# Chaining the second MLP product in PSUM over two quarters, with its finish dealt out and its operand buffers shared

## The chip, the cores and the metric

The kernel runs on one core of a Trainium2 chip. The metric is the device time of one execution in microseconds (us), as the median of several runs.

## What is computed

The reference is one layer of a hybrid diffusion backbone over 2048 tokens of width 1024: token mixing (long convolutions, a state space model, pooling, attention), an output projection, and an MLP. The change concerns the MLP and what ends the layer:

```python
def sq_relu_mlp(h, w1, w2):
    return jnp.square(jax.nn.relu(h @ w1)) @ w2
...
    fl = sq_relu_mlp(modulate(rmsnorm(xl, lp["norm_pre_mlp"]), mod_l[3], mod_l[4]), lp["mlp_w1"], lp["mlp_w2"])
    xl = xl + mod_l[5] * rmsnorm(fl, lp["norm_post_mlp"])
```

Here `h` is 2048 x 1024, `w1` 1024 x 4096 and `w2` 4096 x 1024, all in float32.

## The kernel before

**Precision.** A float32 product is made of three matmuls. `split` (L663) rounds an operand to a high part on ScalarE (L666) and makes the low part by a subtraction on VectorE or GpSimd (L669). `mm3` (L672) issues high x high, high x low and low x high (L674, L675, L676).

**Seven products for eight.** Both MLP products are cut into 2 x 2 blocks and computed with seven block products and additional sums and differences (a Strassen-Winograd scheme). The differences of the weights are made on the chip while the product runs; for the second product the seven left operands are made by the first and kept in DRAM as `m_d`.

**The first product, `mlp_up`** (L1273), runs over two halves of the tokens and 16 chunks each. It holds its right operands as split tiles: `he` (needed early in a chunk, in the pool `hh` on the right side of SBUF) and `hb` (later). TensorE writes PSUM tiles named X, Y, Z; `total` (L1302 to L1304) adds a kept sum on VectorE and squares the positive part on ScalarE. The end of a chunk makes four sums on VectorE (L1361) and writes seven blocks to `m_d` (L1369).

**The output projection, `mix_out`** (L1143), runs before it, block by block of 128 tokens, and its last transposition `turn(7)` is followed by `mlp_up`.

**The second product, `mlp_down`** (L1390). For each half of the tokens and each of eight quarters q of the inner dimension (each 512 deep) it loads two 1 MB pieces of `w2` (`raw`, L1424), makes the differences t1 to t4 (`summed2`, L1493, on VectorE or GpSimd), and calls `product` seven times. `product` loads the left operand (`mr`, L1438), splits it (`ms`) and the weights (`w2s`), and runs 24 matmuls of 128x512: twelve (two token blocks, two 128-deep steps k, three of `mm3`) into each of two PSUM tiles `ps` of two banks. So a quarter has 7 x 24 = 168 matmuls, a half 8 x 168, the stage 2688. Every `ps` is brought out at once: copied by ScalarE in the first quarter (L1450), added to `acc` by VectorE in the others (L1452). Which engine makes which low part is written out in the calls (V is VectorE, G GpSimd).

**The finish.** In the last quarter of a half the seven sums are combined (L1463 to L1486, VectorE and GpSimd), and `finish` (L1404) is called on each y: squares and their sums on ScalarE (L1409), the root by a chain of small VectorE ops (`rsqrt`, L638 to L647), then per 128 tokens a load of x (L1415), the scaling on VectorE (L1416), the addition of x on GpSimd or VectorE (L1417), and the store (L1418).

**Order.** The program is written in the order of these calls; each engine takes its instructions in its own order, and a tile is free when its last reader is done. SP issues all loads and stores of this stage, in order. `psum` has four two-bank tiles in `mlp_down`, and six `ps` and two `pt` one-bank tiles in the stage before it, under separate pools, so the pools of the second product open when those of the first close.

Of the kernel before, what the change touches and what calls it, by code (L numbers as in the profile page):

```python
# [9 lines left out]
F32 = mybir.dt.float32  # L10
F32R = mybir.dt.float32r
# [1131 lines left out]
def mix_out(nc, tc, psum, PI, H, a, C, w, rows_d, cols_d, mT_d, x1_d, h2_d, t_d, raw):  # L1143
# [3 lines left out]
    with tc.tile_pool(name="mo", reuse_waits="tile", bufs=1, side="right") as P:  # L1147
        rows = load(nc, P, rows_d[:, 0], "rows0")
        cols = load(nc, P, cols_d, "colsl")
        def block(blk):  # L1150
            ts = slice(128 * blk, 128 * blk + 128)
            m = PI.tile([128, 8, 128], F32, name="m", bufs=2)
            nc.sync.dma_start(m, mT_d[:, :, ts])
            mh = PI.tile([128, 2, 8, 128], F32R, name="mh", bufs=2)
            split(nc, m, mh[:, 0], mh[:, 1], nc.scalar, V)
            x = P.tile([128, D], F32, name="xr", bufs=2)
            nc.sync.dma_start(x, a["x"][ts])
            ps = [psum.tile([128, 512], F32, tag="ps", name="ps") for _ in range(2)]
            for h in range(2):
                hs = slice(512 * h, 512 * h + 512)  # L1160
                for k in range(8):
                    mm3(nc, ps[h], mh[:, 0, k], mh[:, 1, k], wh[:, k, hs], wl[:, k, hs], k == 0, k == 7)
            rs = P.tile([128, 1], F32, name="ors", bufs=4)
            row_rstd(nc, P, ps, rs, "ro")
            y = P.tile([128, D], F32, name="x1", bufs=2)
            for h in range(2):
                hs = slice(512 * h, 512 * h + 512)
                V.scalar_tensor_tensor(y[:, hs], ps[h], rs, rows[:, hs], op0=ALU.mult, op1=ALU.mult)
            G.tensor_tensor(y, y, x, ALU.add)
            nc.sync.dma_start(x1_d[ts], y)  # L1170
            rs2 = P.tile([128, 1], F32, name="ors2", bufs=4)
            row_rstd(nc, P, [y[:, 0:512], y[:, 512:1024]], rs2, "ro")
            xn = P.tile([128, D], F32, name="xn", bufs=3)
            nc.scalar.activation(xn, y, AF.Copy, scale=rs2)
            return xn

        def turn(t, xs):
            for k in range(0, 8, 2):
                ps = psum.tile([128, 2, 256], F32, tag="pt", name="pt", bufs=2)
                for i in range(2):  # L1180
                    for j in range(2):
                        nc.tensor.transpose(ps[:, i, 128 * j:128 * j + 128], xs[j][:, 128 * (k + i):128 * (k + i) + 128], C["id"])
                for i in range(2):
                    h = P.tile([128, 256], F32, name="h2", bufs=3)
                    nc.scalar.activation(h, ps[:, i], AF.Identity, bias=cols[:, 0, k + i:k + i + 1], scale=cols[:, 1, k + i:k + i + 1])
                    nc.sync.dma_start(h2_d[:, k + i, 256 * t:256 * t + 256], h)

        xs, hb = {}, {}
        for blk in range(16):
            if blk == 12:  # L1190
                for t in raw:
                    nc.sync.dma_start(t[0], t[1])
            xs[blk] = block(blk)
            if blk % 2 == 0 and blk:
                turn(blk // 2 - 1, [xs[blk - 2 + i] for i in range(2)])
            if blk in (9, 10, 11, 12):
                mlp_first(nc, P, H, h2_d, t_d, blk - 9, hb)
# [510 lines left out]
```

## Time and profile before

| | us |
|---|---|
| median of 3 runs | 2978.19 (2974.49 to 2979.24) |
| the profiled execution, its time | 2975.95 |
| its span in the profile | 2974.2 |
| TensorE busy (PE) | 2719.0, 91% |
| VectorE busy (DVE) | 2165.1, 73% |
| GpSimd busy (POOL) | 1512.1, 51% |
| ScalarE busy (ACT) | 1392.7, 47% |
| mean granted clock of TensorE | 0.956 of full speed |

PE is TensorE's matmuls, PEld its weight loads, which overlap them; DVE is VectorE, ACT ScalarE, POOL GpSimd, SP the engine that issues transfers. Busy shares are averages over stages with different limits. The last stage, `mlp_down`, stretches from 2267 to 2974 us. A window row gives, for a stretch of the span, each engine's busy time and its instructions, the granted clock of TensorE (1.00 is 2.4 GHz, 0.50 is 1.2 GHz), the share in which the DMA engines were busy, and the rate. Some per cent of matmul records can be missing from a trace.

### The profile page before, as it was taken

The numbers are of one execution on the slowest core, as the hardware profiler recorded it, in microseconds if no ns is written. First come the engines' busy times: TensorE is split into PE (matmuls) and PEld (weight loads), VectorE is DVE, ScalarE is ACT, GpSimd is POOL, SyncE is SP. The second block draws the span as 40 slices with busy tenths as digits, with TensorE's granted clock in tenths as the row PEclk, the third lists the DMA queues.
The fourth block names the chain that finished last, engine by engine and source line by source line (L and its number), as shares of the span: only waits on it lengthen the run. The fifth ranks groups of instructions, "written<-read, shape, count | busy, mean of one in ns | idle before, by whom it ended". The sixth has DMA issues, their size and how long they took to land.

```text
span 2974.2 us, 38945 instructions
## 1 busy us (share of the span) xinstructions
PE 2719.0 (91%) x13228; PEld 2170.8 (73%) x13228; DVE 2165.1 (73%) x3946; ACT 1392.7 (47%) x2353; POOL 1512.1 (51%) x1334
## 2 busy tenths in 40 slices
PE   7979999978999889989998899999998999889993
PEld 3667778767775785878886677778886888668882
DVE  6867786379776887987677644464445789999997
ACT  5644223234864654647234545565555433353332
POOL 5856887366522622634114354444443555755555
PEclk9988999989999989989999999999999999989997
DMA  6454453253131411412565744464335444455432
GB/s 212 139 176 134 136 153 103 76 161 91 61 108 42 138 41 44 142 56 69 184 215 180 260 170 146 155 212 150 143 144 214 161 145 152 134 193 168 156 121 99
DMA packets 228486, 415.13 MB, mean 140 GB/s; under 512 B 35118, under 2 KB 97394, under 8 KB 226687
## 3 DMA queue, kind: packets, MB, share of 16 engines
q1 hardware_dynamic: 228287, 412.63, 42.7%
q8 instruction: 105, 1.72, 0.2%
q14 instruction: 94, 0.77, 0.1%
HBM read 277.90 MB, written 134.64 MB: 139 GB/s over the span
## 4 chain that ended last, share of the span: by engine, by line
PE 56%; DVE 13%; DMA 5%; issue 3%; ACT 3%; POOL 3%; SPq 0%; DVEq 0%; ACTq 0%; POOLq 0%
PE ps L675 8%; PE ps L676 8%; PE ps L674 8%; PE X L674 3%; PE X L675 3%; PE po L1003 3%; PE X L676 3%; PE pS L916 3%; PE pT L990 3%; PE ps L212 2%; PE Z L674 2%; PE Z L676 2%; PE Z L675 2%; DMA hl<-h_d 1%; DVE pt L669 1%
## 5 line engine op out<-in xcount | busy, mean ns | idle before, releaser
L675 PE MATMUL ps<-w2s,ms 128*128 128x512 f32 x896 | 353.4, 395 | 21.0 <-DVE w2s L669 20.2
L674 PE MATMUL ps<-w2s,ms 128*128 128x512 f32 x896 | 351.4, 395 | 18.0 <-DVE acc L1452 13.4
L676 PE MATMUL ps<-w2s,ms 128*128 128x512 f32 x896 | 351.5, 393 | 1.9 <-POOL ms L669 1.9
L666 ACT ACTIVATE ms<-mr 128x1024 fp32r<-128x1024 f32 x112 | 119.2, 1065 | 324.7 <-issue 146.9
L1452 DVE TENSOR_TENSOR acc<-ps,acc 128x1024 f32<-128x1024 f32 x196 | 234.3, 1214 | 33.4 <-PE ps L676 32.9
L669 POOL TENSOR_TENSOR ms<-mr,ms 128x1024 fp32r<-128x1024 f32 x64 | 162.3, 2536 | 150.7 <-ACT ms L666 150.6
L916 PE MATMUL pS<-KT,QT 128*128 128x512 f32 (+1 forms) x640 | 209.6, 420 | 17.1 <-DVE p L923 13.8
L923 DVE TENSOR_SCALAR_CACHE_REDUCE p<-pS 128x512 f32<-128x512 f32 (+1 forms) x320 | 198.0, 629 | 36.7 <-PE pS L916 34.0
L675 PEld LDWEIGHTS ps<-w2s,ms 128*128 128x128 f32 x896 | 170.7, 191 | 60.6 <-DVE w2s L669 23.0
L930 ACT ACTIVATE p<-p,mx 128x1024 f32<-128x1024 f32 (+1 forms) x192 | 177.4, 927 | 75.8 <-DVE mx L927 75.5
L674 PEld LDWEIGHTS ps<-w2s,ms 128*128 128x128 f32 x896 | 170.4, 190 | 56.4 <-issue 10.5
L669 POOL TENSOR_TENSOR w1s<-w1r,w1s 128x512 fp32r<-128x512 f32 x96 | 133.4, 1391 | 152.9 <-ACT w1s L666 151.3
L666 ACT ACTIVATE pt<-pT 128x512 fp32r<-128x512 f32 x256 | 146.3, 594 | 137.3 <-PE pT L990 119.6
L1003 PE MATMUL po<-pt,VV 128*128 128x256 f32 x1024 | 199.0, 309 | 11.7 <-DVE pt L669 7.0
L676 PEld LDWEIGHTS ps<-w2s,ms 128*128 128x128 f32 x896 | 170.6, 190 | 38.2 <-POOL ms L669 2.8
L990 PE MATMUL pT<-ident,p 128*128 128x128 f32 x1152 | 181.6, 279 | 9.9 <-DVE pt L669 4.6
L669 DVE TENSOR_TENSOR pt<-pT,pt 128x512 fp32r<-128x512 f32 x256 | 171.7, 683 | 18.1 <-ACT pt L666 16.4
L1003 PEld LDWEIGHTS po<-pt,VV 128*128 128x128 f32 x1024 | 154.1, 197 | 41.2 <-DVE pt L669 14.2
L669 DVE TENSOR_TENSOR w1s<-w1t,w1s 128x512 fp32r<-128x512 f32 x128 | 103.4, 810 | 110.0 <-ACT w1s L666 109.2
L990 PEld LDWEIGHTS pT<-ident,p 128*128 128x128 f32 x1152 | 138.6, 143 | 37.4 <-issue 18.0
L669 DVE TENSOR_TENSOR w2s<-w2t,w2s 128x1024 fp32r<-128x1024 f32 x64 | 135.5, 2117 | 25.8 <-ACT w2s L666 25.3
L1302 DVE TENSOR_TENSOR mu<-Z,pk 128x512 f32<-128x512 f32 x64 | 44.1, 690 | 146.1 <-ACT pk L1297 116.8
(484 smaller groups left out, 7767.8 us busy)
## 6 DMA issues: line engine op xcount, KB each, us to landing
mr<-m_d SPq DMA_DIRECT2D x112, 512.0 KB
w1r<-mlp_w SPq DMA_DIRECT2D x64, 512.0 KB
m_d<-mt SPq DMA_DIRECT2D x128, 256.0 KB
w2r<-mlp_w SPq DMA_DIRECT2D x32, 1024.0 KB
mw<-mod_w SPq DMA_DIRECT2D x96, 256.0 KB
m_d<-mu SPq DMA_DIRECT2D x96, 256.0 KB
kk<-k_d SPq DMA_DIRECT2D x128, 128.0 KB
hl<-h_d SPq DMA_DIRECT2D x48, 256.0 KB
```

The costliest lines, as they stand in the source:

```text
L212: nc.tensor.matmul(ps, lhsT=d1[0:64], rhs=zq[:, :, 16 * j:16 * j + 16].rearrange("p t c -> p c t"), start=True, stop=True)
L666: nc.scalar.activation(hi, src, AF.Copy)
L669: lo_eng.tensor_tensor(lo, src, hi.bitcast(F32), ALU.subtract)
L674: nc.tensor.matmul(out, lhsT=lh, rhs=rh, start=start, stop=False, skip_group_check=onto)
L675: nc.tensor.matmul(out, lhsT=lh, rhs=rl, start=False, stop=False, skip_group_check=onto)
L676: nc.tensor.matmul(out, lhsT=ll, rhs=rh, start=False, stop=stop, skip_group_check=onto)
L916: nc.tensor.matmul(s[:, :n], lhsT=QT[:, h, i], rhs=KT[j][:, :n], start=i == 0, stop=i == 1)
L923: V.tensor_scalar(p[:, c0:c0 + n], s[:, :n], 1.0, -3.0e38, op0=ALU.mult, op1=ALU.max, accum_out=mx[:, j:j + 1])
L930: nc.scalar.activation(p[:, :n], p[:, :n], AF.Exp, bias=mx[:, 5:6], accum_out=sm[:, j:j + 1])
L990: nc.tensor.transpose(tp[:, b, h], pr[h][c][:, 128 * i:128 * i + 128], C["id"])
L1003: nc.tensor.matmul(o, lhsT=VV[kb], rhs=pt[:, i, b], start=kb == 0 and i == 0, stop=kb == NB - 1 and i == 1)
L1452: V.tensor_tensor(acc[p][j], ps, acc[p][j], ALU.add)
```

## The change

`mlp_down` is written anew; the places around it change with its buffers.

- Two quarters are one pair. A product is four one-bank sums of 128x512, each chained in PSUM over both quarters of the pair (24 matmuls each where it stood at 12). Four banks are X and four are Z, all eight together; products 0, 5, 6, 3 go into X, products 1, 4, 2 into Z, and some continue a sum that is there (0, 5, 6, 3 and 4, 2 chain), so that several sums of the scheme come out of PSUM ready made. A sum is then copied by ScalarE (L1493, first pair) or added by VectorE (L1495), in pieces of 128x512.
- All low parts, all differences of weights (`minus`, L1435) and the whole finish of half 0 are on VectorE.
- The finish is a generator: `square_sum` (L1440, L1441), `root` (L1447, L1448) and `result` (L1463) per 128 tokens. Half 0's finish is handed out in half 1's first pair, three steps behind each product. Half 1's upper rows are finished between its last products, with the multiplications on GpSimd; its lower rows go block by block in the last product (`outer=True`, `after=end`).
- Operands of both products are `he` tiles from one pool of eight of [128, 2, 2, 512]; the left operands are loaded into `w1r` tiles on both sides of SBUF, the weights in 512 KB pieces.
- In `mix_out` the pool `mo` stays open, `turn(7)` is called in `mlp_up` behind the first two chunks' `begin` and `middle`, the first two `block`s of W1 are put into tiles of `mo`, and h is loaded in pairs.

The core of the diff:

```diff
-    with tc.tile_pool(name="mo", reuse_waits="tile", bufs=1, side="right") as P:
...
-        turn(7, [xs[14 + i] for i in range(2)])
-        return hb
+    return hb, lambda: turn(7, [xs[14 + i] for i in range(2)])
...
     for c in range(2):
         begin(c)
         middle(c)
+    left()
...
+    bank = lambda tag, b: psum.tile([128, 512], F32, tag=tag, name="acc" + tag, bufs=b)
+    pt = [psum.tile([128, 2, 256], F32, tag="pt", name="pt", bufs=2).rearrange("p a b -> p (a b)") for _ in range(2)]
+    ps = [psum.tile([128, 512], F32, tag="ps", name="ps") for _ in range(6)]
+    X, Z = pt + ps[0:2], ps[2:6]
 
-    def block(src, name, lo):
-        w = Q.tile([128, 2, 2, 512], F32R, name=name, bufs=3)
-        split(nc, src, w[:, 0], w[:, 1], A, lo)
+    def block(src):
+        w = H.tile([128, 2, 2, 512], F32R, name="he", bufs=8)
+        split(nc, src, w[:, 0], w[:, 1], A, V)
         return w
...
+    def m_block(half, p, q):
+        t = RW[loads[0] // 2 % 2].tile([128, 8, 128], F32, name="w1r", bufs=2).rearrange("p a b -> p (a b)").rearrange(
+            "p (k n) -> p k n", k=2)
+        loads[0] += 1
+        nc.sync.dma_start(t, m_d[half, p, :, 2 * q:2 * q + 2])
+        return t
...
+    def finish(half, t, acc, xs=(None,) * 4, eng=V):
+        ss = Q.tile([128, 2, 4], F32, name="mss", bufs=2)
+        for b in range(4):
+            for h in range(2):
+                square_sum(acc[t, h][b], ss[:, h, b:b + 1], h, eng)
+            yield
+        rs = root(ss, 4, "4")
+        for b in range(4):
+            result(1024 * half + 512 * t + 128 * b, [acc[t, h][b] for h in range(2)], rs[:, b:b + 1], xs[b])
+            yield
...
+            def product(p, w, dst, start, keys, outer=False, after=None):
+                ms = [None, None]
+                ws = [None, None]
+                steps = [(b, i) for b in range(4) for i in range(2)] if outer else [(b, i) for i in range(2) for b in range(4)]
+                for b, i in steps:
+                    if ms[i] is None:
+                        ms[i] = block(m_block(half, p, qs[i]))
+                        ws[i] = block(w[i])
+                    ts = slice(128 * b, 128 * b + 128)
+                    m, u = ms[i], ws[i]
+                    for k in range(2):
+                        mm3(nc, dst[b], m[:, 0, k, ts], m[:, 1, k, ts], u[:, 0, k], u[:, 1, k],
+                            start and i == 0 and k == 0, i == 1 and k == 1, not start)
+                    if i == 1:
+                        for key in keys:
+                            add(key, dst, b)
+                        if after:
+                            after(b)
+                for _ in range(3 if half == 1 and pair == 0 else 2):
+                    next(rest, None)
+
+            b11 = [w_block(q, 0, 0) for q in qs]
+            product(0, b11, X, True, [(0, 0)])
+            b21 = [w_block(q, 1, 0) for q in qs]
+            product(1, b21, Z, True, [(0, 0)])
...
+            product(5, t2, X, False, [(0, 1)])
+            product(4, t1, Z, True, [(1, 1)])
...
+                product(6, t3, X, False, [(1, 1)])
+                product(2, b22, Z, False, [(0, 1)])
+                product(3, t4, X, False, [(1, 0)])
+        if half == 0:
+            rest = both(finish(half, 0, acc), finish(half, 1, acc))
...
-    with pool("hh", side="right") as H, pool("w1r", side="right") as RW, pool("psC", bufs=6, space=PS) as psum:
+    with pool("w1r", side="right") as RW, pool("hh", side="right") as H, pool("psC", bufs=6, space=PS) as psum:
...
-    with pool("dr", side="right") as R, pool("md") as Q, pool("psD", bufs=4, space=PS) as psum:
-        mlp_down(nc, tc, psum, R, Q, a, rows_d, x1_d, m_d, a["out"])
...
+                with pool("md") as Q:
+                    mlp_down(nc, tc, psum, (RW, RQ), RQ, H, Q, a, rows_d, x1_d, m_d, a["out"])
```

TensorE's order where the first product ends and the second begins. Before, the last chunk's Z is done before the first `ps` (the operands of the second product are w2s and ms):

```order
L674 MATMUL Z<-hb,w1s 128x512
L675 MATMUL Z<-hb,w1s 128x512
L676 MATMUL Z<-hb,w1s 128x512
L674 MATMUL ps<-w2s,ms 128x512 x4
L675 MATMUL ps<-w2s,ms 128x512
L676 MATMUL ps<-w2s,ms 128x512
```

No matmul of the second product stands ahead of the first product's last. Now the new product's matmuls on `pt` and `ps`, with both operands in `he`, stand before the last chunk's X:

```order
L674 MATMUL pt<-he 128x512
L675 MATMUL pt<-he 128x512
L676 MATMUL pt<-he 128x512
L674 MATMUL ps<-he 128x512
L675 MATMUL ps<-he 128x512
L676 MATMUL ps<-he 128x512
L674 MATMUL X<-hb,w1s 128x512
L675 MATMUL X<-hb,w1s 128x512
L676 MATMUL X<-hb,w1s 128x512
```

Fifteen matmuls of the second product stand there, and further ones between the last X, X and Z of the first: 37 ahead of its last matmul.

VectorE's order where half 0 ends and half 1 begins. Before, in the last quarter of half 0, the combination and `finish` (L1476, L1481, L1410, L642) stand in one place with the accumulations:

```order
L669 TENSOR_TENSOR ms<-mr,ms 128x1024
L669 TENSOR_TENSOR w2s<-w2t,w2s 128x1024
L1452 TENSOR_TENSOR acc<-ps,acc 128x1024 x3
L1476 TENSOR_TENSOR y<-y,acc 128x2x512
L1481 TENSOR_TENSOR acc<-acc 128x1024
L1452 TENSOR_TENSOR acc<-ps,acc 128x1024
L1476 TENSOR_TENSOR y<-y,acc 128x2x512
L1410 TENSOR_SCALAR mss<-mss 128x2
L1481 TENSOR_TENSOR acc<-acc 128x1024
L1452 TENSOR_TENSOR acc<-ps,acc 128x1024
L642 TENSOR_SCALAR rmt<-mss 128x2
```

The splits of ms and w2s for the next products follow these rows. Now the multiplications of the finish (L1441) stand between additions and splits of half 1's first products:

```order
L669 TENSOR_TENSOR he<-w1r,he 128x1024
L1495 TENSOR_TENSOR acc<-ps,acc 128x512
L669 TENSOR_TENSOR he<-w2a,he 128x1024
L1495 TENSOR_TENSOR acc<-ps,acc 128x512
L1441 TENSOR_TENSOR acc<-acc,rows_21765 128x512
L1495 TENSOR_TENSOR acc<-ps,acc 128x512
L1441 TENSOR_TENSOR acc<-acc,rows_21765 128x512
L1495 TENSOR_TENSOR acc<-ps,acc 128x512
L1441 TENSOR_TENSOR acc<-acc,rows_21765 128x512
L669 TENSOR_TENSOR he<-w1r,he 128x1024
L669 TENSOR_TENSOR he<-w2a,he 128x1024
L1441 TENSOR_TENSOR acc<-acc,rows_21765 128x512 x4
```

The ops of the finish have moved from half 0's last quarter to half 1's first products, one to four at a time between the splits of `he`.

At the program's end VectorE now has the addition, the multiplication and the root chains of single blocks, two chains interleaved, and the fused multiply-adds (L1463) behind them:

```order
L1495 TENSOR_TENSOR acc<-ps,acc 128x512
L1441 TENSOR_TENSOR acc<-acc,rows_21765 128x512
L1448 TENSOR_SCALAR mv_26042<-mv_26042 128x1
L642 TENSOR_SCALAR rm1t<-mv_26007 128x1
L1441 TENSOR_TENSOR acc<-acc,rows_21765 128x512
L642 TENSOR_SCALAR rm1t<-mv_26042 128x1
L643 TENSOR_SCALAR mrs_26008<-rm1t 128x1
L643 TENSOR_SCALAR mrs_26043<-rm1t 128x1
```

The addition of the last of the four blocks is followed by two chains for two blocks; the other two blocks' chain and their L1463 come behind the first pair's.

## Rows read from the trace of the kernel before

**Rows 1.** The page's busy times of each engine over the whole span.

```profile
PE 2719.0 (91%) x13228; PEld 2170.8 (73%) x13228; DVE 2165.1 (73%) x3946; ACT 1392.7 (47%) x2353; POOL 1512.1 (51%) x1334
```

**Rows 2.** Windows: stretch, engines' busy time and instructions, clock, DMA share, GB/s.

```profile
2263.00:2304.00 41.00, 28.81 (x106) 21.69 (x105) 22.68 (x13) 22.18 (x24) 20.37 (x8) 0.83 0.64 236
2304.00:2560.00 256.00, 256.00 (x1132) 212.01 (x1131) 222.49 (x157) 100.20 (x100) 133.50 (x55) 1.00 0.48 155
2560.00:2680.00 120.00, 92.70 (x370) 73.32 (x369) 116.22 (x103) 52.01 (x61) 82.47 (x29) 0.87 0.47 167
...
2928.70:2974.20 45.50, 0.14 (x1) 0.00 (x0) 35.90 (x68) 7.20 (x14) 13.43 (x5) 0.54 0.44 162
```

**Rows 3.** Timeline of TensorE's last matmuls: start, duration, engine, line, tiles.

```profile
2925.73 0.39 PE L676 MATMUL ps<-w2s,ms 128*128 128x512 f32 x1
...
2928.45 0.39 PE L676 MATMUL ps<-w2s,ms 128*128 128x512 f32 x1
```

**Rows 4.** The page's costliest groups: busy, mean ns, idle before, releaser.

```profile
L675 PE MATMUL ps<-w2s,ms 128*128 128x512 f32 x896 | 353.4, 395 | 21.0 <-DVE w2s L669 20.2
...
L666 ACT ACTIVATE ms<-mr 128x1024 fp32r<-128x1024 f32 x112 | 119.2, 1065 | 324.7 <-issue 146.9
L1452 DVE TENSOR_TENSOR acc<-ps,acc 128x1024 f32<-128x1024 f32 x196 | 234.3, 1214 | 33.4 <-PE ps L676 32.9
```

**Rows 5.** Timeline of the entry into the second product, all engines.

```profile
2262.89 0.39 PE L676 MATMUL Z<-hb,w1s 128*128 128x512 f32 x1
2263.32 0.69 DVE L1302 TENSOR_TENSOR mu<-Z,pk 128x512 f32<-128x512 f32 x1 [0.41 <-PE Z L676]
...
2264.71 0.63 ACT L1304 ACTIVATE mu<-mu 128x512 f32<-128x512 f32 x1
...
2266.70 2.86 DVE L1361 TENSOR_TENSOR mt<-mu 128x512 f32<-128x512 f32 x1
...
2267.28 1.22 PE L674 MATMUL ps<-w2s,ms 128*128 128x512 f32 x2 [4.00 <-ACT w2s L666]
...
2272.26 1.21 DVE L669 TENSOR_TENSOR ms<-mr,ms 128x1024 fp32r<-128x1024 f32 x1
...
2273.40 1.21 DVE L669 TENSOR_TENSOR w2s<-w2r,w2s 128x1024 fp32r<-128x1024 f32 x1
...
2274.67 0.80 PE L675 MATMUL ps<-w2s,ms 128*128 128x512 f32 x1 [4.26 <-DVE w2s L669]
```

**Rows 6.** Waits in 2555 to 2690: who waits for what, us, times, longest.

```profile
PE ps L674 <- DVE acc L1452: 13.4, 4, 9.2
PE ps L675 <- DVE w2s L669: 12.7, 3, 7.3
```

**Rows 7.** Timeline of VectorE at the half boundary.

```profile
2619.33 6.66 DVE L1416 SCALAR_TENSOR_TENSOR y<-y,mrs,rows 128x1024 f32<-128x1024 f32 x2
...
2643.92 3.44 DVE L669 TENSOR_TENSOR ms<-mr,ms 128x1024 fp32r<-128x1024 f32 x1
```

**Rows 8.** Timeline behind the last matmul.

```profile
2946.72 0.16 DVE L646 SCALAR_TENSOR_TENSOR rmt<-rmt,mrs 128x2 f32<-128x2 f32 x1
2946.91 0.16 DVE L647 SCALAR_TENSOR_TENSOR mrs<-rmt,mrs 128x2 f32<-128x2 f32 x1
...
2966.53 2.34 POOL L1417 TENSOR_TENSOR y<-y,xf 128x1024 f32<-128x1024 f32 x1 [4.64 <-DMA xf<-x_d]
...
2969.20 1.23 DVE L1417 TENSOR_TENSOR y<-y,xf 128x1024 f32<-128x1024 f32 x1 [5.10 <-DMA xf<-x_d]
```

**Rows 9.** Timeline of TensorE in the first product, two moving operands.

```profile
2109.74 0.39 PE L674 MATMUL Z<-hb,w1s 128*128 128x512 f32 x1
...
2112.46 0.40 PE L674 MATMUL X<-he,w1s 128*128 128x512 f32 x1
...
2120.86 0.39 PE L674 MATMUL X<-hb,w1s 128*128 128x512 f32 x1
```

More of the change, by code (lines that the diff above doesn't have):

```diff
@@ L1140, in load_w_out, with mix_out @@
     return wh, wl
-def mix_out(nc, tc, psum, PI, H, a, C, w, rows_d, cols_d, mT_d, x1_d, h2_d, t_d, raw):
+def mix_out(nc, P, psum, PI, H, a, C, w, rows_d, cols_d, mT_d, x1_d, h2_d, t_d, raw):
     V, G = nc.vector, nc.gpsimd
     wh, wl = w
-    with tc.tile_pool(name="mo", reuse_waits="tile", bufs=1, side="right") as P:
[L1148 to L1197, printed above, removed]
-        turn(7, [xs[14 + i] for i in range(2)])
-        return hb
@@ L1202 @@
+    xs, hb = {}, {}
+    for blk in range(16):
+        if blk == 12:
+            for t in raw:
+                nc.sync.dma_start(t[0], t[1])
+        xs[blk] = block(blk)
+        if blk % 2 == 0 and blk:
+            turn(blk // 2 - 1, [xs[blk - 2 + i] for i in range(2)])
+        if blk in (9, 10, 11, 12):
+            mlp_first(nc, P, H, h2_d, t_d, blk - 9, hb)
+    return hb, lambda: turn(7, [xs[14 + i] for i in range(2)])
 EARLY = ("a", "c", "t2", "t1")
@@ L1281, in operand @@
         if n not in hb[half]:
-            hb[half][n] = mlp_operand(nc, Q, H if n in EARLY else late(), h2_d, t_d, half, n)
+            hb[half][n] = mlp_operand(nc, HL, H if n in EARLY else late(), h2_d, t_d, half, n)
         return hb[half][n]
     def block(src, lo):
-        w = Q.tile([128, 2, 4, 128], F32R, name="w1s", bufs=4)
+        if first:
+            w = first.pop().tile([128, 2, 512], F32R, name="hl", bufs=2).rearrange("p s (k n) -> p s k n", k=4)
+        else:
+            w = Q.tile([128, 2, 4, 128], F32R, name="w1s", bufs=4)
         split(nc, src, w[:, 0], w[:, 1], A, lo)
@@ L1292, in product @@
         for k in range(4):
-            mm3(nc, ps, w[:, 0, k], w[:, 1, k], h[k][:, 0], h[k][:, 1], start and k == 0, k == 3, not start)
+            hk = h[k // 2][:, :, k % 2]
+            mm3(nc, ps, w[:, 0, k], w[:, 1, k], hk[:, 0], hk[:, 1], start and k == 0, k == 3, not start)
     def keep(ps):
@@ new lines, in minus, with square_sum, root @@
+    def minus(x, y, t=None):
+        if t is None:
+            t = Q.tile(B3, F32, name="w2t", bufs=4)
+        V.tensor_tensor(t, x, y, ALU.subtract)
+        return t
+    def square_sum(y, ss, h, eng=V):
+        sq = Q.tile([128, 512], F32, name="msq", bufs=1)
+        A.activation(sq, y, AF.Square, accum_out=ss)
+        eng.tensor_tensor(y, y, rows[:, 512 * h:512 * h + 512], ALU.mult)
+    def root(ss, n, tag):
+        v = Q.tile([128, n], F32, name="mv" + tag, bufs=2)
+        rs = Q.tile([128, n], F32, name="mrs" + tag, bufs=2)
+        V.tensor_tensor(v, ss[:, 0], ss[:, 1], ALU.add)
+        V.tensor_scalar(v, v, 1.0 / D, EPS, op0=ALU.mult, op1=ALU.add)
+        rsqrt(nc, Q, v, rs, n, "rm" + tag)
+        return rs
@@ new lines, in x_rows, with result @@
+    def x_rows(t0, x=None):
+        if x is None:
+            x = Q.tile([128, D], F32, name="xf", bufs=3)
+        nc.sync.dma_start(x, x1_d[t0:t0 + 128])
+        return x
+    def result(t0, y, rs, x=None):
+        ts = slice(t0, t0 + 128)
+        x = x_rows(t0) if x is None else x
+        for h in range(2):
+            hs = slice(512 * h, 512 * h + 512)
+            V.scalar_tensor_tensor(x[:, hs], y[h], rs, x[:, hs], op0=ALU.mult, op1=ALU.add)
+        nc.sync.dma_start(out[ts], x)
+    def finish(half, t, acc, xs=(None,) * 4, eng=V):
+        ss = Q.tile([128, 2, 4], F32, name="mss", bufs=2)
+        for b in range(4):
+            for h in range(2):
+                square_sum(acc[t, h][b], ss[:, h, b:b + 1], h, eng)
[4 more added lines that the diff above has]
+            yield
```

229 lines of the change are left out of this document (121 added, 108 removed).

## The prediction

> **What bounds the kernel now.** I read the page's engine table first [rows 1]: TensorE is busy 91% of the span and no other engine over 73%, so time can only be won where TensorE stands idle, or by cheaper matmuls. The kernel's other stages are left almost as they are, so next I cut the second MLP product into windows [rows 2]. From 2304 to 2560 us it has no gap: TensorE is busy all 256 us at the full clock. Its pace is read at the end of the stage [rows 3]: twelve matmuls from 2925.73 to 2928.45, 0.2267 us each. The stage has 2688 of them (three groups of 896, [rows 4]). So what the change takes from VectorE, ScalarE or GpSimd inside that window is worth nothing: it was already hidden behind matmuls.
>
> What is not hidden are three places.
> - The entry. Window 2263 to 2304 holds 106 matmuls, worth 106 x 0.2267 = 24.0 of 41 us: **17.0 us** lost. The last Z matmul starts at 2262.89, the first of the product 4.4 us later, after ScalarE's rounding of w2s; after four matmuls TensorE waits 4.26 us for VectorE's low part, because VectorE still finishes the first product's sums, with ops stretched to 2.86 us [rows 5]. The window's granted clock is 0.83 [rows 2], so some of its matmuls ran at the lower level, 1.2 GHz.
> - The half boundary, 2560 to 2680: 370 matmuls x 0.2267 = 83.9 of 120 us, **36.1 us** lost. VectorE is busy 116.2 of the 120 us, and the two largest waits of TensorE's matmuls both are for it: 13.4 us for an accumulation, 12.7 for a w2s low part [rows 6]. The accumulations and splits that feed TensorE stand among the ops of `finish`, and beside GpSimd's work a split of 1.21 us [rows 5] takes 3.44, and two ops of L1416 take 6.66 [rows 7].
> - The tail: after the last matmul **45.5 us** with TensorE idle [rows 2]. VectorE's last addition waits 5.10 us for a load of x and ends at 2970.43 [rows 8]; the output's transfer closes the span 3.8 us later, at 2974.2.
>
> Together 98.6 us; this is what the change can reach.
>
> **The change, part by part.**
>
> *Chaining in PSUM, 512-column sums (L1493/1495).* Two quarters are summed in PSUM before they leave it, so VectorE's 196 additions of 128x1024 at 1.21 us (234 us, [rows 4]) become 28 of 128x512 per pair of quarters. VectorE's price for such an addition out of PSUM is 0.69 us, that of the op on mu [rows 5]. In the gap-free windows this is worth 0. It counts for the boundary.
>
> *Subtractions and low parts on VectorE alone.* Per pair of quarters there are 28 splits and 8 subtractions at 1.14 us from start to start (2272.26 to 2273.40, [rows 5]) = 41 us, and 28 additions x 0.69 = 19 us: 60 of the 336 x 0.2267 = 76 us that TensorE needs. GpSimd is silent, so nothing stretches these ops. ScalarE has 28 roundings x 1.065 = 30 us [rows 4]. In the first pair, 16 of the additions are ScalarE copies. Cost 0, hidden behind TensorE; without that cover it would be the 16 us of slack that is missing.
>
> *The entry.* The operands now go into the buffers that the first product used, and the order of TensorE shows the join: 15 matmuls of the new product stand before the first product's X, 37 before its last Z. They need the first product's early operands gone, which are long done there. VectorE still has the same last sums to make, and SP still writes the last m blocks; but TensorE has 37 x 0.2267 = 8.4 us of its own work there, and GpSimd no longer stretches the ops. I keep 4 us of the 17.0, with bounds 0 and 17: **-13.0**.
>
> *The half boundary.* Half 0's `finish` is 16 multiplications and 16 fused multiply-adds of 128x512 at 0.69 = 22 us, two root chains of 13 small ops at 0.19 [rows 8] = 5 us and 8 loads and 8 stores, three of its sixteen steps behind each product, so over six products. VectorE's load in half 1's first pair is then 41 + 8 (12 additions) + 22 + 5 = 76 of 76 us: just full, but spread, with no op over 1.21 us ahead of one that TensorE needs. On SP a store that waits for VectorE stands before the next loads of m; four w1r buffers, two products, are the lead. I keep 4 of the 36.1, bounds 0 and 36: **-32.1**.
>
> *The tail.* Half 1's first row half is finished under the last products, with GpSimd's eight multiplications (an op of twice that size takes it 2.34 us where VectorE is idle, [rows 8]) behind the last 10.9 us of matmuls. The last product goes block by block; of its four blocks one is left when TensorE stops. Then: matmul end 0.4, addition 0.7, square on ScalarE about 1.0 (a 128x512 one takes 0.63, [rows 5], and its sum must be read), multiplication 0.7, two interleaved root chains of 13 small ops, 0.19 apart, 2.5, four fused ops of 0.7 = 2.8, the second pair's chains 2.3, four fused ops 2.8, output 3.8 [rows 8]: 17.0 us. No x load stands in it, they were issued a product earlier. Bounds 12 and 25: 17.0 - 45.5 = **-28.5**.
>
> *The operand buffers.* This is the part that costs. In the first product the same instruction with the same shape runs at two paces, by its moving operand [rows 9]: with `hb` twelve matmuls from 2109.74 to 2112.46 take 2.72 us, 0.2267 each; with `he`, the next thirty-six, to 2120.86, take 8.40 us, 0.2333 each. Now both operands of all 2688 matmuls of the second product are `he`. 2688 x 0.0066 = **+17.7**. In the built program the `he` tiles begin 32 bytes past a multiple of 64, `hb`, `ms` and `w2s` on one, before and after; I take this as the likely reason, but the sum uses only the buffer. Bounds: 0 if the buffer is not what matters, 35 if a weight loaded from `he` costs as much again; weight loads have only ever come from w1s and ms in these two stages, so no row shows that, and I take the row there is.
> The Trainium skill, "TensorE: Matmul & The Clock Gate", section "Back-to-back issue gap", has a gap that depends on the columns alone (512 at full clock: some 216 ns); by it the two paces should be one and this term 0. The trace does not agree with it on that.
>
> *Outside the product.* The first two W1 blocks are put into another buffer, `turn(7)` moves behind the first two chunks, the mix pool lives longer and h loads go in pairs. The same work on the same engines; bounds -8 and +8, taken at 0.
>
> **Sum.** The profiled execution took 2975.95 us (span 2974.2 and 1.75 around it). 2975.95 - 13.0 - 32.1 - 28.5 + 17.7 = 2920.05, so **2920**. That run lies 2.2 us under the median of the runs shown, so against the median the gain is 58.
>
> **The rivals.**
> (a) *The pace does not follow the buffer.* Against: the alternation is clean. For: it is seen only where `he` is the moving operand of the first product. 2920 - 17.7 = **2902**. Chance 0.12.
> (b) *The stalls stay.* VectorE is exactly full in half 1's first pair, and a `finish` that waits for its squares can hold what is queued behind it. If entry and half boundary keep half of their losses beyond what I left (6.5 + 16), 2942; if all, 2965. Chance 0.12; I name **2950**.
> (c) *The four sums hand over badly.* Product 3 of a pair and product 0 of the next both write X, as do 6 and 3 in the last pair, so the next chain starts on a bank whose addition may not be done. Per handover four additions of 0.69 = 2.8 us, eight handovers: +22, **2942**. Against: the first bank's chain ends 18 matmuls = 4.1 us before the last's, long enough for 0.69 each if VectorE is free. Chance 0.09. The Trainium skill, "Perfetto Trace Analysis", section "Matmuls" under "Optimizing Tensor Performance", advises rotating independent groups through PSUM banks so that emptying one overlaps the next; here all eight banks are in the four sums and nothing spare is left to rotate into, and by that rule this rival would be the case.
> (d) *Slower: the shared ring leaves no lead.* A product takes four of the eight `he` buffers, so operands for the next can only be made while one runs. If they come late, each of 56 products waits for a rounding and a low part, 1.06 + 1.21 = 2.27 us: +127, **3047**. It decides against the gain from 55.9 / 56 = 1.0 us per product. Against: making four operands takes VectorE 4.6 us and ScalarE 4.3 of a product's 10.9. Chance 0.03.
> (e) *Nothing reachable*: each stall is replaced by one of its size, and the result is within 0.2% (6 us, about what a measurement of this kernel can tell from no change). Chance 0.02, **2976**.
>
> **The numbers.** Forecast 0.62, (a) 0.12, (b) 0.12, (c) 0.09, (d) 0.03, (e) 0.02. The range reaches down to (a) and 5 us of the tail's lower bound, 2897, and up past (b)'s middle, 2953; outside lie the worse half of (b), (d), (e) and the ends of the unknowns added up. Faster by over 0.2%: 0.95; same 0.02; slower 0.03.
>
> **What would show it.** Right: matmuls of the second product 0.233 us apart throughout; no idle of TensorE over 2 us at the join or at half 1's start; VectorE near full only in half 1's first pair; some 17 us after the last matmul; GpSimd's w2s, ms and w2t groups gone. Wrong: matmuls 0.227 apart (a); TensorE waiting for `he` low parts around the middle of the stage (b); regular gaps of 1 to 3 us at each pair's first matmul, released by L1495 (c); a wait at every product (d).

## The result and the profile after

The changed kernel takes 2900.98 us (median of 4 runs, 2896.35 to 2902.28) against 2978.12 us: a ratio of 0.974, with a 95% interval of 0.9723 to 0.9757. It is 77 us faster; 2920 had been forecast, with a range of 2897 to 2953. The profiled execution took 2896.35 us (span 2894.4), the fastest of the four.

The page's busy times of the engines, whole span, which answer to [rows 1]:

```profile
PE 2706.1 (93%) x13228; PEld 2162.6 (75%) x13228; DVE 2043.7 (71%) x4063; ACT 1386.2 (48%) x2369; POOL 1130.4 (39%) x1192
```

GpSimd has lost 382 us of work, VectorE 121, and TensorE's busy time hardly moved. Where the time went is seen in windows of the last stage (columns as in [rows 2]):

```profile
2244.00:2304.00 60.00, 54.31 (x228) 43.66 (x227) 43.84 (x45) 28.95 (x39) 2.13 (x1) 0.94 0.76 265
2304.00:2560.00 256.00, 256.00 (x1131) 212.06 (x1130) 195.05 (x209) 100.98 (x108) 0.00 (x0) 1.00 0.51 154
...
2560.00:2680.00 120.00, 120.00 (x531) 99.38 (x530) 104.59 (x144) 61.81 (x86) 0.00 (x0) 1.00 0.67 221
2680.00:2876.40 196.40, 196.40 (x867) 162.27 (x865) 149.38 (x175) 74.81 (x90) 11.74 (x8) 1.00 0.41 123
2876.40:2894.40 18.00, 0.02 (x1) 0.00 (x0) 14.34 (x68) 2.89 (x8) 0.00 (x0) 0.56 0.38 154
```

- The entry: 228 matmuls x 0.2267 = 51.7 of 60 us, 8.3 lost, where it was 17.0. Two waits hold most of it; TensorE's timeline shows them (in brackets the idle time before, and who ended it):

```profile
2284.20 0.73 PE L674 MATMUL pt<-he 128*128 128x512 f32 x2 [3.82 <-ACT he L666]
...
2287.65 0.79 PE L675 MATMUL pt<-he 128*128 128x512 f32 x1 [1.87 <-DVE he L669]
```

- From 2304 to the last matmul TensorE has no gap: at the half boundary 0 is lost, where it was 36.1. VectorE is busy 104.6 of 120 us there, so it was not full.
- Behind the last matmul 18.0 us, where it was 45.5. VectorE's work there fell from 35.9 us [rows 2] to 14.3. Its groups for the scaling and the addition of x, two of before and two of now (busy, mean ns of one, idle before):

```profile
L1416 DVE SCALAR_TENSOR_TENSOR y<-y,mrs,rows 128x1024 f32<-128x1024 f32 x8 | 12.0, 1539 | 0.0
L1417 DVE TENSOR_TENSOR y<-y,xf 128x1024 f32<-128x1024 f32 x4 | 4.9, 1218 | 5.1 <-DMA xf<-x_d 5.1
...
L1463 DVE SCALAR_TENSOR_TENSOR w2r<-acc,mrs,w2r 128x512 f32<-128x512 f32 x8 | 5.5, 747 | 0.0
L1441 DVE TENSOR_TENSOR acc<-acc,rows 128x512 f32<-128x512 f32 x4 | 2.7, 686 | 0.1
```

Before, all eight blocks of 128 tokens of half 1 were scaled behind the last matmul; now only the four lower ones are, and nothing waits for x.

Together the three places are 72 of the 80 us between the two spans. Of the other 8, some 2 are gaps that were there between 2680 and 2928.7 us and are gone, and 5 lie before the MLP (the first product starts at 1595.5 instead of 1600.3); that part is no effect to explain, since in the runs below, whose kernels do not differ there, it starts anywhere from 1594 to 1604.

The pace is the surprise. Timeline of TensorE, first in the first product, then in the second (two matmuls each, eighteen and twenty-four apart; start, duration):

```profile
2003.18 0.40 PE L674 MATMUL X<-he,w1s 128*128 128x512 f32 x1
...
2007.38 0.40 PE L676 MATMUL X<-he,w1s 128*128 128x512 f32 x1
...
2700.11 0.39 PE L674 MATMUL ps<-he 128*128 128x512 f32 x1
...
2705.55 0.39 PE L674 MATMUL ps<-he 128*128 128x512 f32 x1
```

With w1s as weights and `he` moving, a matmul still takes 0.2333 us; with `he` on both sides it takes 5.44 / 24 = 0.2267. The term of +17.7 us did not come.

VectorE's operations are no longer stretched; the groups of the splits and the additions in 2520 to 2640 us (busy, mean ns of one, idle before):

```profile
L669 DVE TENSOR_TENSOR he<-w1r,he 128x1024 fp32r<-128x1024 f32 x23 | 28.1, 1220 | 8.1 <-ACT he L666 8.1
...
L1495 DVE TENSOR_TENSOR acc<-ps,acc 128x512 f32<-128x512 f32 x24 | 16.0, 684 | 0.1
```

Where a split took up to 3.4 us at the boundary before [rows 7], it now takes 1.22 on average.

### The profile page after: what moved, and what is told of

Same layout as the page of the kernel before. It is cut to its first block, busy times and chain, and to the rows that moved or that the text cites. A ratio compares the mean times of both kernels' runs of the same rounds, so it can differ in the third digit from the quotient of the medians.

```text
span 2894.4 us, 38905 instructions
## 1 busy us (share of the span) xinstructions
PE 2706.1 (93%) x13228; PEld 2162.6 (75%) x13228; DVE 2043.7 (71%) x4063; ACT 1386.2 (48%) x2369; POOL 1130.4 (39%) x1192
## 4 chain that ended last, share of the span: by engine, by line
PE 59%; DVE 11%; DMA 4%; ACT 3%; issue 3%; POOL 1%; SPq 0%; DVEq 0%; ACTq 0%; POOLq 0%
PE ps L676 7%; PE ps L675 7%; PE ps L674 7%; PE X L674 4%; PE X L676 3%; PE X L675 3%; PE po L1003 3%; PE pS L916 3%; PE pT L990 3%; PE ps L212 2%; PE pt L675 2%; PE pt L676 2%; PE pt L674 2%; PE Z L674 2%; PE Z L675 2%
## 5 line engine op out<-in xcount | busy, mean ns | idle before, releaser
L666 ACT ACTIVATE he<-w1r 128x1024 fp32r<-128x1024 f32 x112 | 118.8, 1061 | 312.4 <-PE ps L676 285.2
L675 PE MATMUL ps<-he 128*128 128x512 f32 x640 | 249.0, 389 | 0.0
L676 PE MATMUL ps<-he 128*128 128x512 f32 x640 | 248.2, 389 | 0.0
L1441 POOL TENSOR_TENSOR acc<-acc,rows 128x512 f32<-128x512 f32 x8 | 11.7, 1487 | 604.2 <-ACT msq L1440 604.2
L674 PE MATMUL ps<-he 128*128 128x512 f32 x640 | 245.5, 390 | 0.0
L669 DVE TENSOR_TENSOR he<-w1r,he 128x1024 fp32r<-128x1024 f32 x112 | 137.8, 1230 | 113.6 <-ACT he L666 113.3
L1318 POOL TENSOR_TENSOR w1t<-w1r 128x512 f32<-128x512 f32 x64 | 86.7, 1355 | 156.2 <-DMA w1r<-mlp_w 110.8
L916 PEld LDWEIGHTS pS<-KT,QT 128*128 128x128 f32 x640 | 103.7, 193 | 48.0 <-DVE p L923 24.5
L674 PEld LDWEIGHTS ps<-he 128*128 128x128 f32 x640 | 120.3, 188 | 24.9
L676 PEld LDWEIGHTS ps<-he 128*128 128x128 f32 x640 | 120.2, 188 | 25.0
```

The lines of the kernel that those rows point to most:

```text
L666: nc.scalar.activation(hi, src, AF.Copy)
L669: lo_eng.tensor_tensor(lo, src, hi.bitcast(F32), ALU.subtract)
L674: nc.tensor.matmul(out, lhsT=lh, rhs=rh, start=start, stop=False, skip_group_check=onto)
L675: nc.tensor.matmul(out, lhsT=lh, rhs=rl, start=False, stop=False, skip_group_check=onto)
L676: nc.tensor.matmul(out, lhsT=ll, rhs=rh, start=False, stop=stop, skip_group_check=onto)
L916: nc.tensor.matmul(s[:, :n], lhsT=QT[:, h, i], rhs=KT[j][:, :n], start=i == 0, stop=i == 1)
```

## The experiments

What stood to be settled: why the pace is 0.2267 in the second product; which part of the change closed the entry, the half boundary and the tail; and whether something is left. All edits are to the changed kernel unless said otherwise, and times are medians, against its 2901. The kernel before, run again beside each set of runs, had medians from 2978.3 to 2981.3 us, so a difference of 3 us between sets says nothing by itself.

### The pace: where operands begin in SBUF

```diff
-    with pool("w1r", side="right") as RW, pool("hh", side="right") as H, pool("psC", bufs=6, space=PS) as psum:
+    with pool("pad", side="right") as PD, pool("w1r", side="right") as RW, pool("hh", side="right") as H, pool("psC", bufs=6, space=PS) as psum:
+        PD.tile([128, 8], F32, name="pad")
```

> 32 bytes are put at the right end of SBUF ahead of the two right-hand pools, so that the he tiles begin on a multiple of 64 instead of 32 past one. Theory A (a matmul costs 0.0066 us more where its weights and its moving operand begin at different places modulo 64): the first product's he matmuls, 1536, go from 0.2333 to 0.2267 us, -10 us, about 2891; the second product stays at 0.2267. Theory B (the moving operand's place alone costs, and something in the second product hides it): the same -10 us here. Theory C (the pace belongs to the buffer or the stage, not to addresses): he stays at 0.2333, 2901.

Measured: 2897.05 us (ratio 0.9727, 0.9705 to 0.9749), and `he` with w1s stays at 0.2333 (4.20 us for eighteen):

```profile
2005.39 0.39 PE L674 MATMUL X<-he,w1s 128*128 128x512 f32 x1
...
2009.59 0.39 PE L676 MATMUL X<-he,w1s 128*128 128x512 f32 x1
```

Both A and B fall as they were put: a multiple of 64 is not it.

The other way round, the first product's left-hand pools were moved:

```diff
-                with pool("mu") as Q, ExitStack() as more:
+                with pool("pad") as PD, pool("mu") as Q, ExitStack() as more:
+                    PD.tile([128, 8], F32, name="pad")
```

> The opposite way: 32 bytes are put ahead of the first product's left-hand pools, so that w1s and hb also begin 32 past a multiple of 64, like he. Theory A: all three match, he matmuls go to 0.2267 us and hb stay there, -10 us, about 2891. Theory B: he stays at 0.2333 and the 1152 hb matmuls join it, +7.6 us, about 2909. Theory C: nothing moves, 2901.

Measured: 2902.13 us (0.9738, 0.9723 to 0.9754); `he` 0.2333, `hb` unchanged. On these two alone theory C would stand.

Then the weights of the second product were moved inside their buffers, which grow by 64 bytes for it:

```diff
+def he_tile(P, off):
+    t = P.tile([128, 2064], F32R, name="he", bufs=8)
+    return t[:, off:off + 2048].rearrange("p (s k n) -> p s k n", s=2, k=2)
...
-                        ms[i] = block(m_block(half, p, qs[i]))
+                        ms[i] = block(m_block(half, p, qs[i]), 8)
```

> In the second product the left operands (the weights of its matmuls) are put 32 bytes further into their he buffers, so that weights begin on a multiple of 64 and moving operands 32 past one; the small mv and mrs tiles of the four-block roots lose their second buffer to make room. Theory A: 2688 matmuls go from 0.2267 to 0.2333 us, +17.7 us, about 2919. Theories B and C: 2901, pace unchanged.

Measured: 2918.06 us (0.9789, 0.9765 to 0.9813), +17.1, the size that A had. Twenty-four matmuls of the second product now take 5.59 us, 0.2329 each:

```profile
2700.04 0.39 PE L676 MATMUL ps<-he 128*128 128x512 f32 x1
...
2705.63 0.39 PE L676 MATMUL ps<-he 128*128 128x512 f32 x1
```

So it is the relation of the two operands after all, and C falls. In the built programs the starts of the operands then say how far the relation reaches. The pairs that are fast lie at the same place modulo 512 (w1s and `hb` both at 0, and both at 32 in the second run; ms and w2s of the kernel before at 0; both `he` at 480, and at 448 in the first run). The slow ones do not: `he` begins 480 past w1s as built, 448 past it in the first two runs. The third run was not a shift of 32 bytes alone: in the larger buffers the two operands of its second product lie 224 apart modulo 512. The next two runs were made on that; their edits are shown against the first run's.

```diff
-        PD.tile([128, 8], F32, name="pad")
+        PD.tile([128, 24], F32, name="pad")
```

> 96 bytes instead of 32 ahead of the right-hand pools. The earlier runs fit one rule: the slow pace comes where weights and moving operand begin at different places modulo M, with M one of 128, 256, 512 (the weights of one tile differ by multiples of 512 and all keep one pace). Here he and w1s differ by nothing modulo 128, by 128 modulo 256. If M is 128, the first product's he matmuls go to 0.2267 us; if M is 256 or 512, they stay at 0.2333; if the rule is wrong, they stay too, and so they do with 480 bytes.

Measured, in a single run: 2895.35 us, `he` against w1s 4.19 us for eighteen, 0.2328. It stays slow: being equal modulo 128 is not enough.

```diff
-        PD.tile([128, 8], F32, name="pad")
+        PD.tile([128, 120], F32, name="pad")
```

> 480 bytes ahead of the right-hand pools: he, hb and w1s begin at the same place modulo 512. By the rule, whatever M, all matmuls of the first product go to 0.2267 us, 1536 x 0.0066 = 10 us less, about 2891. If the pace belongs to the buffer after all (left-hand weights against a right-hand operand), 2901 and 0.2333.

Measured: 2892.47 us (0.9722, 0.97 to 0.9744; 5 runs), 8.5 us under the changed kernel. The two intervals overlap, and two kernels above that stayed slow, with 32 and 96 bytes, were 4 and 6 us under it too; so it is the trace that shows the gain: from its first matmul to its last the first product takes 663.9 us (1598.28 to 2262.16) where the changed kernel takes 671.1 (1595.53 to 2266.59). The timeline shows the step itself, 4.08 us for eighteen, 0.2267 each:

```profile
2003.32 0.39 PE L674 MATMUL X<-he,w1s 128*128 128x512 f32 x1
...
2007.40 0.39 PE L676 MATMUL X<-he,w1s 128*128 128x512 f32 x1
```

The rule holds in the two MLP products of all seven kernels read for it: 0.2267 us where weights and moving operand begin at the same place modulo 512, 0.2333 where they do not. No run has a difference of 256, so whether being equal modulo 256 would do is not told apart; other stages were not tried.

### The join

The second product gets a PSUM pool of its own, which opens when the first product's closes:

```diff
+                sums.close()
-                with pool("md") as Q:
+                with pool("md") as Q, pool("psD", bufs=6, space=PS) as psum:
                     mlp_down(nc, tc, psum, (RW, RQ), RQ, H, Q, a, rows_d, x1_d, m_d, a["out"])
```

> The second product takes its eight banks from a pool that opens when the first product's closes, as before the change, so none of its matmuls stands ahead of the first product's last. Theory (the join hides part of the entry): TensorE loses 11 to 17 us between the products instead of the changed kernel's 7, so +4 to +10 us, 2905 to 2911. Rival (the join only moves the wait, the operands come when they come): within 2 us of 2901.

Measured: 2902.29 us (0.9738, 0.972 to 0.9756): no difference. A split for the second product, a wait of the first product, its last matmul and the second's first, in the timeline:

```profile
2261.50 1.21 DVE L669 TENSOR_TENSOR he<-w2a,he 128x1024 fp32r<-128x1024 f32 x1
...
2268.91 0.50 PE L674 MATMUL X<-hb,w1s 128*128 128x512 f32 x1 [2.80 <-ACT pk L1306]
...
2275.91 0.39 PE L676 MATMUL Z<-hb,w1s 128*128 128x512 f32 x1
...
2277.08 0.50 PE L674 MATMUL pt<-he 128*128 128x512 f32 x1 [0.78 <-DVE mu L1311]
```

1.2 us lie between the matmuls: the operands are ready, since their splits (such as the one at 2261.50) run beside the first product. TensorE now waits 2.80 us inside the first product for ScalarE's copy `pk`, where matmuls of the second product stood, and behind the join the two waits for `he` (3.82 and 1.87 us) are gone. So the 37 matmuls ahead do fill waits, but the time is lost again behind them, and in sum they are worth nothing, as the rival had it. That the operands come early because they go into shared buffers fits this, but the sharing was not taken away by itself.

### GpSimd

GpSimd again makes the low parts of the left operands of four of the seven products:

```diff
-    def block(src):
+    def block(src, lo=V):
...
-        split(nc, src, w[:, 0], w[:, 1], A, V)
+        split(nc, src, w[:, 0], w[:, 1], A, lo)
...
-                        ms[i] = block(m_block(half, p, qs[i]))
+                        ms[i] = block(m_block(half, p, qs[i]), (nc.gpsimd, V)[p % 2])
```

> In the second product GpSimd again makes the low parts of the left operands of products 0, 4, 2 and 6, 64 in all, as before the change. Theory (GpSimd beside VectorE stretched the ops that TensorE waited for): VectorE's ops of 1.21 us show up to 3.4 us again, and TensorE waits for he at the entry and in half 1's first pair, 3 to 12 us more, 2904 to 2913; elsewhere hidden. Rival (with VectorE's additions halved there is room for the stretching): within 2 us of 2901.

Measured: 2906.80 us (0.9766, 0.9746 to 0.9785), +5.8. The groups of VectorE's splits in 2300 to 2888 us:

```profile
L669 DVE TENSOR_TENSOR he<-w2r,he 128x1024 fp32r<-128x1024 f32 x32 | 69.6, 2176 | 11.1 <-ACT he L666 10.8
L669 DVE TENSOR_TENSOR he<-w2t,he 128x1024 fp32r<-128x1024 f32 x45 | 66.3, 1474 | 1.1 <-ACT he L666 1.1
```

The mean of 2176 ns (1217 without) is a mix of undisturbed and stretched ops, from 1210 to 3428. At the half boundary 120 us hold 513 matmuls, 116.3 us of work, so 3.7 are lost there; the theory's size is right. The entry's two waits are as long as without the edit, and a third of 1.2 us, for a low part of GpSimd, has joined them.

The converse is the kernel before the change with all low parts and weight differences on VectorE and nothing else changed:

```diff
-        split(nc, src, w[:, 0], w[:, 1], A, lo)
+        split(nc, src, w[:, 0], w[:, 1], A, V)
...
-            ws = lambda x, y, eng: summed2(nc, R, x, y, eng)
+            ws = lambda x, y, eng: summed2(nc, R, x, y, V)
```

> The kernel before the change, with all low parts and all weight differences of the second product on VectorE; its finish keeps GpSimd. Theory (the change's parts need each other: without chaining VectorE is full): per two quarters it has 36 x 1.14 + 28 x 1.21 = 75 us of work for 76 of matmuls, so there is no slack for the finish; the half boundary keeps some 35 us of loss or more and the middle loses a little, 2975 to 3000. Rival (the stretching by GpSimd was the whole cause): the boundary's loss falls below 15 us and the entry's too, 2945 to 2960.

Measured: 2945.44 us (0.99, 0.9877 to 0.9923), 33 us less than the kernel before. My theory was wrong, the rival right. Its windows:

```profile
2250.00:2300.00 50.00, 42.63 (x178) 33.91 (x177) 31.82 (x32) 29.39 (x36) 0.23 (x1) 0.93 0.83 309
2263.00:2304.00 41.00, 34.37 (x142) 27.86 (x143) 27.66 (x26) 27.18 (x29) 0.00 (x0) 0.92 0.76 280
2300.00:2540.00 240.00, 240.00 (x1060) 198.74 (x1059) 224.28 (x197) 93.97 (x95) 0.00 (x0) 1.00 0.48 154
2540.00:2680.00 140.00, 129.55 (x557) 104.89 (x556) 138.58 (x148) 68.41 (x77) 32.63 (x10) 0.99 0.52 173
...
2898.70:2943.70 45.00, 0.17 (x1) 0.00 (x0) 34.78 (x68) 6.99 (x14) 13.32 (x5) 0.53 0.47 163
```

The entry, in the stretch of [rows 2], loses 41 - 142 x 0.2267 = 8.8 us instead of 17.0, the half boundary 140 - 557 x 0.2267 = 13.7 instead of 36.1, the tail 45.0 as before. VectorE is busy 93% of the middle and TensorE still has no gap: here an engine that is nearly full costs nothing while its ops keep their length. A stretched split took 3.44 us [rows 7], about 1.21 of its own and one GpSimd op of 2.34 [rows 8]. The Trainium skill, "SBUF — State Buffer", section "Who interferes with whom", says that VectorE and GpSimd share a port pair as an exclusive lock; by that an op can wait for a whole op of the other engine, and the trace agrees with it.

### Chaining

Every sum that leaves PSUM is read once more by VectorE:

```diff
                     V.tensor_tensor(acc[key][b], src[b], acc[key][b], ALU.add)
+                V.bn_stats(Q.tile([128, 6], F32, name="again", bufs=2), src[b])
```

> Every sum that leaves PSUM is read by VectorE a second time into a scratch tile (224 statistics ops of 128x512, 0.68 us each, 19 us per pair of quarters), about what leaving PSUM after every quarter would cost. Theory (chaining over two quarters is what lets VectorE carry the rest alone): VectorE has 58 of 76 us of work in an ordinary pair and 66 in half 1's first, so 77 and 85: TensorE waits some 9 us there and 1 per other pair, 2910 to 2920. Rival (VectorE's slack is worth nothing, reads of PSUM lie off the path): 2901 within 3. By my sum of before the run VectorE was just full in half 1's first pair: then +19 there alone and 3 per other pair, 2938.

Measured: 2939.34 us (0.9869, 0.985 to 0.9888), +38. The windows of the stage:

```profile
2304.00:2560.00 256.00, 251.25 (x1105) 206.79 (x1104) 235.58 (x287) 98.77 (x106) 0.00 (x0) 1.00 0.50 151
2560.00:2680.00 120.00, 107.55 (x449) 86.42 (x448) 117.82 (x174) 55.50 (x82) 0.00 (x0) 0.94 0.62 202
2680.00:2914.00 234.00, 231.29 (x1017) 190.35 (x1016) 217.34 (x277) 88.89 (x109) 12.49 (x8) 1.00 0.41 121
```

By counted matmuls it loses 5.5, 18.2 and 3.4 us there, and 4.7 more behind the last matmul. Its waits in 2560 to 2660 us show what holds TensorE (us, times, longest):

```profile
PE ps L674 <- DVE again L1496: 6.1, 3, 4.2
...
PE pt L674 <- DVE again L1496: 3.5, 1, 3.5
...
PE ps L675 <- DVE he L669: 2.1, 1, 2.1
```

A matmul waits for the second reading of its bank: the extra reads do not only load VectorE, they keep banks. The busy share does not tell this: in the first window VectorE is busy 92% and TensorE loses 5.5 us, where it lost none at 93% in the run above. So this kernel, with all eight banks in use, does not bear twice the reading of PSUM. What it would lose without chaining is not shown: then a bank would be read once each time and not held longer, and the run above, which has no chaining, has no gap in the middle. The size agrees with my sum of before the run, and not with the smaller one made from VectorE's busy share; that agreement may be chance, since the waits are partly for banks, which neither sum had.

### How the finish is written

```diff
-            rest = both(finish(half, 0, acc), finish(half, 1, acc))
+            for _ in both(finish(half, 0, acc), finish(half, 1, acc)):
+                pass
```

> Half 0's finish is written in one piece at the end of half 0 instead of in steps behind the products of half 1. Theory (the order in which VectorE gets the ops is nearly the same either way, and its slack carries them): 2901 within 3, no gap of TensorE at half 1's start. Rival (the dealing out is what closed the half boundary): 10 to 35 us more, 2911 to 2936, with waits of TensorE for he low parts around 2580 to 2640.

Measured: 2900.06 us (0.9737, 0.9712 to 0.9762): no difference. In 2560 to 2680 us it loses nothing either:

```profile
2560.00:2680.00 120.00, 120.00 (x531) 99.43 (x530) 103.36 (x142) 63.56 (x91) 0.00 (x0) 1.00 0.65 219
```

The built program has the finish of half 0 at the same places of half 1 either way: VectorE's order differs only in where three ops (two splits, one weight difference) stand by a few places, SP's in where a few loads stand, and TensorE's and ScalarE's not at all. Where the source writes these ops does not decide where they run, so dealing them out in the source is worth nothing. What a finish that really ran in one piece would cost, this run does not show.

```diff
-                product(6, t3, X, False, [(1, 1)], after=lambda b: square_sum(acc[1, 1][b], ss[:, 1, b:b + 1], 1))
+                product(6, t3, X, False, [(1, 1)])
...
-                for _ in rest:
-                    pass
-                product(3, t4, X, False, [(1, 0)], outer=True, after=end)
+                product(3, t4, X, False, [(1, 0)])
+                for _ in both(rest0, finish(half, 1, acc, xs)):
+                    pass
```

> The changed kernel without its block-by-block end: product 3 of the last pair is written like the others, the lower rows' finish in one piece behind it, with one root for four blocks; the upper rows' finish is written there too, with GpSimd's multiplications. Theory (one root chain of 2.5 us instead of two pays for the multiplications that are left): the time behind the last matmul stays at 16 to 21 us, against 18.4, so 2899 to 2904. Rival (going block by block is what shortened the end): 8 to 15 us more, 2909 to 2916.

Measured: 2899.46 us (0.9738, 0.9715 to 0.976), no difference; 16.6 us from the end of the last matmul to the end of the span. One root chain for four blocks pays for the multiplications that remain. So block by block is not what made the tail short. Here too the upper rows' finish runs ahead of the last matmul, and the multiply-adds are fused; what each of these is worth no run separates.

### A better version

```diff
-        nc.sync.dma_start(t, w2[q, s, :, :, 512 * h:512 * h + 512])
+        (nc.gpsimd if h and first_pair[0] else nc.sync).dma_start(t, w2[q, s, :, :, 512 * h:512 * h + 512])
...
+    first_pair = [True]
...
+            first_pair[0] = False
...
+        PD.tile([128, 120], F32, name="pad")
```

> The changed kernel with 480 bytes ahead of the right-hand pools and with the first pair's four second-column weight loads issued by GpSimd, which is idle there, instead of behind SP's last m stores. Theory (TensorE's wait of 4.2 us at the entry is for the differences of these weights, which land late because SP issues them behind stores that wait for VectorE): the loads start some 5 us sooner, the two gaps of 4.2 and 2.0 us shrink to under 2 together, about 4 to 5 us less than with the 480 bytes alone, 2887 to 2889. Rival (the loads wait for the first product's buffers anyway): 2892.

Measured: 2891.23 us (0.9717, 0.9692 to 0.9742; 480 bytes included): 1.2 us under the padding alone, less than the runs of one kernel differ. The transfers did start earlier, one at 2252.6 and three from 2261.7 on instead of all from 2272.6 on, and landed at most 6.6 us after their issue. TensorE's second wait is gone, but it still waited 4.6 us in one piece; so the loads were not the main cause. VectorE's timeline in this run shows what stands in front:

```profile
2273.52 0.69 DVE L1496 TENSOR_TENSOR acc<-ps,acc 128x512 f32<-128x512 f32 x1 [4.68 <-PE ps L676]
2274.88 0.69 DVE L1496 TENSOR_TENSOR acc<-ps,acc 128x512 f32<-128x512 f32 x1 [0.67 <-PE ps L676]
2276.24 0.69 DVE L1496 TENSOR_TENSOR acc<-ps,acc 128x512 f32<-128x512 f32 x1 [0.67 <-PE ps L676]
2276.85 1.22 DVE L1436 TENSOR_TENSOR w2t<-w2r,w2a 128x1024 f32<-128x1024 f32 x1
```

The weight differences (L1436 here) stand behind three additions of product 1, which wait for TensorE, while VectorE is idle for 4.68 us before the first of them, and the last of the weights had landed by 2270. That this order is the cause is read from the trace: putting the differences ahead of these additions was not tried.

## Why the prediction was right or wrong

- **What the change can reach: right.** Window by window, the three places named hold 72 of the 80 us; the gap-free middle gave nothing, as said.
- **The half boundary (-32.1): right in place, -36.1 measured, but two of its reasons fell.** VectorE was forecast to be just full in half 1's first pair, 76 of 76 us; it was busy 66.9 of the 76.3 us from 2571.7 to 2648.0, because part of the finish had run before. "Spread, with no op over 1.21 us ahead of one that TensorE needs" was credited to the steps behind the products; the ops are spread, but the run with the finish written in one piece has them in the same places, so the steps do not do it. Taking GpSimd's low parts and differences out alone is worth 22 of the 36 in the kernel before. The 14 left went with the rest of the change, and no run says with which part: the doubled reads show 18 coming back when VectorE's reads of PSUM double, which is not the same as no chaining.
- **The entry (-13.0): -8.7 measured, with one of its two reasons.** "GpSimd no longer stretches the ops" holds: its absence alone gives 8.2 us in the kernel before. The 8.4 us of TensorE's own work ahead of the join are in sum worth nothing. Of what is left, 8.3 us, 5.7 are two waits that the change has put there; by the trace they are for differences queued behind additions. The sum kept 4 us for all that and did not ask what stands ahead of the differences in VectorE's queue.
- **The tail (-28.5): right, -27.5.** The order of ops and their prices held: from the end of the last matmul 18 us against 17. Two of its reasons are seen in the trace: half of the blocks are finished ahead of the last matmul, and no load of x stands in it. That going block by block contributes was wrong: the run without it is as fast.
- **The operand buffers (+17.7): the step that failed.** "Now both operands are `he`" was counted as the slow case, since in the first product a moving `he` is slow. What counts is where the two operands begin relative to each other, and with both in one pool they agree. The rows [rows 9] hold only pairs with w1s, so they could not tell the two apart. Rival (a), that the pace does not follow the buffer, at 2902, was this case; it had 0.12. So 2901 lies in the range because the range was drawn down to this rival. The guess beside the term, that beginning on a multiple of 64 is the reason, was wrong too; it was near, since the reason is where operands begin.
- **Rivals (b), (c), (d).** No stall at the half boundary, no wait at a pair's handover, and no lead lost: TensorE has no gap from 2304 us to its last matmul. All eight banks are in the sums, and yet nothing waits; only when each bank is read twice do waits for banks appear, so (c) describes a limit that is near.

The profiled execution lies 23.7 us under the forecast of 2920.05: 17.7 by the buffers, 7.5 outside the three places, most of it a start of the first product that differs from run to run, 4.0 by the half boundary; the entry gave 4.3 less than forecast and the tail 1.0 less. That the three gains add up to 72.3 where 73.6 had been forecast is in part luck, since the misses of the entry and the boundary cancel.

## What to carry to other kernels

When an edit takes work off a second engine, look first at what that engine does to the length of the first one's ops: here moving the work to the fuller engine alone was worth 33 us, and in the middle of the stage the fuller engine cost TensorE nothing at 93% busy. Price a stall by who stands in front of the awaited op in its engine's queue, not by when its data arrive. And where one matmul shape runs at two paces, compare the addresses of both operands before blaming the buffer.

## What the runs showed of the hardware that I had not expected

- A 128x512 matmul with 128 weight columns takes 0.2267 us at the full clock where weights and moving operand begin at the same place modulo 512 bytes in their partition, and 0.2333 where they do not (3%). Moving the 1512 slow matmuls of the first product from the one to the other by 480 bytes of padding made that product 7.2 us shorter; moving 2688 the other way cost 17.1.
- VectorE's 128x1024 split takes 1.22 us with GpSimd silent and up to 3.44 beside it.
